# A list schedule that also holds the first stage, counts transfers by bytes and by how many are under way, and uses durations from a trace

## The chip, the cores and the metric

The kernel runs on one core of a Trainium2 chip. The metric is the device time of one execution in microseconds (us); lower is better. Engines: PE is TensorE, DVE VectorE, ACT ScalarE, POOL GpSimd, SP the engine that here only issues DMAs.

## The reference

One transformer layer of width 1024 on 1024 rows, batch 1, all in float32:

```python
u = rms_norm(h, g_norm_mix)
proj = einsum('btd,de->bte', u, w_in) + b_in
mq, mk, mv, mo, mi, mf, nq, nkv, ngate, merge = split_columns(proj, IN_SIZES)
y_m = mlstm_mixer(mq, mk, mv, mo, mi, mf, ...)      # 4 heads of 128, chunks of 128 rows
y_n = nsa_mixer(nq, nkv, ngate, pe_cmp, w_cmp1, w_cmp2, rel_bias)   # 8 heads of 64
branch = einsum('btnw,nwd->btnd', stack([y_m, y_n]), w_branch)
h = h + sum(sigmoid(merge) * branch) @ w_out
f = rms_norm(h, g_norm_ffn)
h = h + (silu(f @ w_gate) * (f @ w_up)) @ w_down
return rms_norm(h, g_final)
```

The mLSTM mixer puts a causal convolution of width 4 and a silu on q and k, works in 8 chunks per head with a running state, and multiplies each score by a decay that depends on the row, the column and the gates. The second mixer has compressed keys and values (blocks of 32 rows, stride 16, through a small two-layer network), selected blocks and a window, with a bias by distance.

## The kernel before, in words

**Products.** A float32 product is made from two halves: each operand is split into a high part (rounded) and the rest, and three matmuls (high·high, low·high, high·low; L343, L344, L345) are summed in PSUM. ACT writes the high part, DVE the low one.

**First stage (L413 to L577), written out by hand.** x comes in 8 tiles of 128 rows. norm(i) squares a tile and sums it on ACT (L458), works out the row's scale in a few one-column instructions (L353 to L360) and scales the tile on DVE (L462; in two halves for tiles 0 and 1). trans(i) transposes it in 8 matmuls of 128x128 (L467) into one PSUM tile and splits that into UTH and UTL (L340 is the low half): u, transposed, is what all later products read. p0(i) multiplies the tile by 288 columns of w_in in 24 matmuls. Those columns are 256 of V, 24 and 8 gate columns (MI); their weights come in 9 loads of SP, three for each group of rows (the tiles named raw), and are split in L325. p0_out adds the bias. The code of the loop at L546 fixes the order on every engine: trans(i+1), p0_out(i-1), norm(i+3), p0(i).

**The plan (class at L60, used from L583).** From there on nothing is in hand order. Code describes steps: on which engine, at which cost in ns, what buffers it reads and writes. Plan.run then picks, again and again, the step that can start first among the first few of each engine's list (the older one at a tie), by its own clocks, and issues it. The engines keep that order: each executes its own row of instructions, and waits in it. A step that depends on another engine's can start 190 ns (HOP) after its end, on PE another 500 ns (slack) later. A DMA costs SP 60 ns and lands a fixed 2,600 ns later (others 2,200 to 9,000), however large it is and however many are under way.

**What the plan holds.** The rest of the first stage (p0 of tile 7, and mv: the tile by 512 columns); twelve pairs of 128-column projections (PAIRS), each as seven products of 12 matmuls (Strassen's scheme, L343 to L345 with output bk), whose operands are formed in L703 and split in L594 and whose results are added up in L758 and L761; after each "qk" pair one mLSTM head; the gates; rel_rows (eight copies of a bias row to 128 partitions, d_rep, 960 KB each); compress.

**A head (L1030).** masks(cp) for each of four pairs of chunks loads two rows by row index, copied to 128 partitions: M from d_M and S from d_S (L1050, 128 KB each). L1052 makes the causal mask of M, L1054 copies the pair's decay out of S, another instruction scales q by S. st_a(c) is the score product (L1062) with an Exp on ACT and the product of both on DVE (L1072); st_b(c) holds the state's product (L1081) and the two of the output, pn (L1091, L1093). The pairs share two buffers: the load of pair 2 waits for the last reader of pair 0. When all chunks are done, norm_1 and norm_3 (L1116 to L1134, 11 small instructions), a scaling of the whole head (L594, RND) and 8 transposes on PE (L1144) follow. Mask rows, norm rows and the operands of later products stand in one row on DVE.

**Compress.** Two halves j. KX holds one half's keys in two shifted copies, loaded from d_kc by four DMAs (L1179, L1180); DVE and ACT copy strided columns of it out (L1196), which L1202 multiplies. The second half's load waits until the first half's copies have read KX, the first one's until the masks' buffers are free.

**After the plan** (PE from about 412 us on) come the attention, the merge and the FFN.

Of the kernel before, what the change touches and what calls it, by code (L numbers as in the profile page):

```python
# [65 lines left out]
class Plan:  # L66
# [4 lines left out]
    def __init__(self, banks, look=None, slack=0.0, **clock):  # L71
        self.LOOK, self.slack = look or self.LOOK, slack
        self.clock = dict({"PE": 0.0, "ACT": 0.0, "DVE": 0.0, "Pool": 0.0, "SP": 0.0}, **clock)
        self.todo = {e: [] for e in self.clock}
        self.at, self.n, self.boost = {}, 0, 0
        self.banks = [[ap, None] for ap in banks]
# [10 lines left out]
    def step(self, alts, fn, reads=(), writes=(), lat=0.0, after=0.0):  # L87
        deps = {d for b in reads for d in b.w} | {d for b in writes for d in b.w + b.r}
        for b in writes:
            if not b.w:  # L90
                for p in b.prior:
                    p.over = True
                    deps |= set(p.w + p.r)
        if any(b.over for b in (*reads, *writes)):
            raise RuntimeError("a region is used after it was given away")
        st = Step(alts, fn, deps, writes, lat, self.n - self.boost, after)
        self.n += 1
# [20 lines left out]
    def ready(self, st, eng, free, first):  # L118
        t = st.after
# [43 lines left out]
def body(ctx, tc, a, out):  # L163
# [16 lines left out]
    nc.scalar.activation(warm, eps, AF.Sqrt)  # L180
# [87 lines left out]
    d_M = tc.dram_tile([32, P], F32, name="d_M")  # L268
    d_S = tc.dram_tile([32, P], F32, name="d_S")
# [159 lines left out]
    BV = RMV()[:, 0:512]  # L429

    def load_x(i):
        nc.sync.dma_start(XS[i % 4], a["x"][P * i:P * i + P, :])

    load_x(0)
    load_x(1)
    nc.scalar.dma_start(gB, a["g_norm_mix"].partition_broadcast(P))
    nc.scalar.dma_start(cst, a["cst"].rearrange("p (n c) -> p n c", n=2))
    bin_ = a["b_in"]
    ws.dma(j_p0[-1])
    load_x(2)  # L440
    load_x(3)
    nc.gpsimd.dma_start(BB[:, 0:128], bin_[C_VS:C_VS + P].partition_broadcast(P))
    nc.gpsimd.dma_start(BB[:, 128:280], bin_[C_VW:C_VW + 152].partition_broadcast(P))
    nc.gpsimd.dma_start(BB[:, 280:288], bin_[C_MI:C_MI + 8].partition_broadcast(P))
    nc.gpsimd.dma_start(BV, bin_[C_MV:C_MV + 512].partition_broadcast(P))
    rv = lambda v, n: v.rearrange("(n c) -> n c", c=P)
    nc.gpsimd.dma_start(rows[0:16, :], rv(bin_[0:2048], 16))
    nc.gpsimd.dma_start(rows[16:20, :], rv(bin_[C_NQ:C_NQ + 512], 4))
    nc.gpsimd.dma_start(rows[20:26, :], rv(bin_[C_KV:C_KV + 768], 6))
    nc.gpsimd.dma_start(rows[26:42, :], rv(bin_[C_MG:C_MG + 2048], 16))  # L450
    nc.gpsimd.dma_start(rows[R_CV:R_CV + 32, :], a["conv_qk"].rearrange("j (n c) -> (j n) c", c=P))
    nc.gpsimd.dma_start(rows[R_GH:R_GH + 4, :], rv(a["g_mlstm_head"], 4))
    nc.gpsimd.dma_start(rows[R_PE:R_PE + 32, :], a["pe_cmp"].rearrange("j (o w) d -> (j o) (w d)", w=2))
    nc.gpsimd.dma_start(BF, a["b_fgate"].partition_broadcast(P))

    def norm(i):
        st, x_ = STA[i % 3], XS[i % 4]
        nc.scalar.activation(SQ, x_, AF.Square, accum_out=st[:, 0:1])  # L458
        rstd(st, D)
        for hf in range(2 if i < 2 else 1):  # L460
            ds_ = slice(512 * hf, 512 * hf + 512) if i < 2 else slice(0, D)
            nc.vector.scalar_tensor_tensor(x_[:, ds_], x_[:, ds_], st[:, 2:3], gB[:, ds_], ALU.mult, ALU.mult)  # L462

    def trans(i):
        pt = psT.tile([P, KT, P], F32, name=f"pt{i}", tag="pt", bufs=2)
        for k in range(KT):
            nc.tensor.transpose(pt[:, k, :], XS[i % 4][:, P * k:P * k + P], ident)  # L467
        if i + 4 < NT:
            load_x(i + 4)
        cs = slice(P * i, P * i + P)  # L470
        split_evict(UTH[:, :, cs], UTL[:, :, cs], pt)

    p0s = {}

    def p0_mm(i, ps):
        cs = slice(P * i, P * i + P)
        for k in range(KT):
            mm3(ps[:, 0:288], UTH[:, k, cs], UTL[:, k, cs], P0H[:, k, :], P0L[:, k, :], k == 0, k == KT - 1)

    def p0(i):  # L480
        p0s[i] = psT.tile([P, 512], F32, name=f"p0_{i}", tag="D", bufs=3)
        p0_mm(i, p0s[i])

    def p0_out(i, ps):
        vt, vs = VT[i % 2], VS[i % 2]
        nc.vector.tensor_tensor(vt, ps[:, 0:256], BB[:, 0:256], ALU.add)
        nc.vector.tensor_tensor(GT[:, i, :], ps[:, 256:288], BB[:, 256:288], ALU.add)
        v4 = vt.rearrange("p (n d) -> p n d", n=4)
        split_evict(vs[:, :, 0:64], vs[:, :, 64:128], v4)

    def mv_mm(i, ps):
        cs = slice(P * i, P * i + P)
        for k in range(KT):
            mm3(ps, UTH[:, k, cs], UTL[:, k, cs], MVW[0][k // 2][:, k % 2, :], MVW[1][k // 2][:, k % 2, :], k == 0, k == KT - 1)

    def mv_out(i, ps):
        nc.vector.tensor_tensor(MVS[i % 2], ps, BV, ALU.add)

    def v_store(i):
        nc.sync.dma_start(d_vhl[:, i], cast32(VS[i % 2]))  # L500

    def mv_store(i):
        nc.sync.dma_start(d_mv[:, :, i], MVS[i % 2].rearrange("p (h d) -> p h d", h=MH))


    RAWP = []
# [1855 lines left out]
```

## Time and profile before

| what | us |
|---|---|
| median of 3 runs | 1604.07 (1602.08 to 1604.45) |
| the profiled execution | 1605.79 |
| its span (first to last instruction) | 1603.9 |
| PE busy in it | 1536.7 |
| DVE, ACT, POOL busy | 1183.8, 785.5, 123.7 |
| first stage, by hand | about 0 to 58 |
| planned part | about 58 to 412 |

The busy time of an engine is the time in which at least one of its instructions ran; PE's instructions overlap, so a product's duration (0.39 us) is longer than its share of PE's time. "Idle before" in a row is the time for which the engine had nothing running, with what ended it: `<-DMA R<-d_M` is a load from d_M into the buffer R.

### The profile page before, as it was taken

Reading aid. Unit: us, or ns where it says so; the run is one execution under the profiler, and the core shown is the slowest. Engines: PE = TensorE matmul, PEld = TensorE weight load, DVE = VectorE, ACT = ScalarE, POOL = GpSimd, SP = SyncE. Lnnn points to the kernel's source line nnn. Section 1 sums busy time; section 2 is a strip of 40 time slices with the busy share of each in tenths; the row PEclk is TensorE's granted clock in tenths of the full one; section 3 lists DMA queues with packets and bytes.
Section 4 is the critical chain, followed back from the end, with each engine's and each line's share of the span. In section 5 each row is a group of like instructions: output and inputs, shape, how many; then the busy total and the mean of one; then the engine's idle time right before and its main releaser. Section 6 shows DMA issues by size and latency. Waiting matters only on the chain.

```text
span 1603.9 us, 22044 instructions
## 1 busy us (share of the span) xinstructions
PE 1536.7 (96%) x7714; PEld 1294.9 (81%) x7714; DVE 1183.8 (74%) x2448; ACT 785.5 (49%) x1664; POOL 123.7 (8%) x181
## 2 busy tenths in 40 slices
PE   6899989898999999998999989999999999999997
PEld 6778767787898988887787878888888888888876
DVE  6878787865798878785554488676576666978996
ACT  5336365553588868885444234333333333454433
POOL 1000000002110301001000022000000000000030
PEclk9999999999999999999999999999999999999999
DMA  6523556479623733217548212222332223741202
GB/s 209 171 75 94 172 173 199 127 193 233 152 58 95 124 85 101 67 33 273 157 138 269 73 66 88 84 80 92 119 92 79 79 79 116 278 162 49 95 11 105
DMA packets 168439, 198.22 MB, mean 124 GB/s; under 512 B 11432, under 2 KB 127590, under 8 KB 168328
## 3 DMA queue, kind: packets, MB, share of 16 engines
q1 hardware_dynamic: 156456, 183.10, 36.4%
q0 software_dynamic: 11536, 13.05, 5.1%
q8 instruction: 61, 1.00, 0.3%
q10 hardware_dynamic: 336, 0.66, 0.1%
q14 instruction: 50, 0.41, 0.1%
HBM read 146.34 MB, written 58.29 MB: 128 GB/s over the span
## 4 chain that ended last, share of the span: by engine, by line
PE 78%; DVE 10%; DMA 6%; ACT 3%; issue 2%; SPq 1%; POOL 0%; DVEq 0%; ACTq 0%
PE PS L344 15%; PE PS L345 15%; PE PS L343 15%; PE T L1498 4%; PE bk L343 3%; PE bk L345 3%; PE bk L344 3%; PE d L343 2%; PE obank L1520 2%; PE obank L1518 2%; PE d L345 2%; PE d L344 2%; PE br L345 2%; PE br L344 1%; PE br L343 1%
## 5 line engine op out<-in xcount | busy, mean ns | idle before, releaser
L1863 DVE TENSOR_TENSOR sl<-PS,sl 128x512 f32<-128x512 f32 x182 | 123.8, 687 | 98.0 <-PE PS L345 96.0
L1507 DVE TENSOR_TENSOR TL<-T,TH 128x512 fp32r<-128x512 f32 (+1 forms) x184 | 103.3, 581 | 28.7 <-ACT TH L1503 27.9
L1503 ACT ACTIVATE TH<-T 128x512 fp32r<-128x512 f32 (+1 forms) x184 | 90.3, 510 | 26.4 <-PE T L1498 23.4
L1863 DVE TENSOR_TENSOR sl<-sl,sl 128x512 f32<-128x512 f32 (+1 forms) x113 | 77.3, 690 | 17.1 <-ACT sl L1866 11.7
L1866 ACT ACTIVATE sl<-sl 128x512 f32<-128x512 f32 (+1 forms) x85 | 53.5, 631 | 70.9 <-PE PS L344 47.8
L343 PE MATMUL bk<-UTH,op 128*128 128x512 f32 x192 | 77.6, 404 | 1.7 <-ACT R L761 1.3
L1866 ACT ACTIVATE wh<-sl 128x512 fp32r<-128x512 f32 x61 | 38.4, 630 | 81.9 <-PE PS L344 71.6
L345 PE MATMUL bk<-UTH,op 128*128 128x512 f32 x192 | 75.1, 391 | 0.4 <-DVE op L594 0.4
L344 PE MATMUL bk<-UTL,op 128*128 128x512 f32 x192 | 75.0, 391 | 0.0
L343 PE MATMUL d<-UTH,whi 128*128 128x512 f32 x176 | 71.9, 408 | 1.3 <-ACT mg L1373 0.7
L345 PE MATMUL d<-UTH,wlo 128*128 128x512 f32 x176 | 69.2, 393 | 1.4 <-POOL wlo L325 1.4
L344 PE MATMUL d<-UTL,whi 128*128 128x512 f32 x176 | 69.0, 392 | 0.0
L343 PE MATMUL PS<-q 128*128 128x512 f32 x172 | 66.9, 389 | 0.0
L344 PE MATMUL PS<-q 128*128 128x512 f32 x172 | 66.9, 389 | 0.0
L345 PE MATMUL PS<-q 128*128 128x512 f32 x172 | 66.9, 389 | 0.0
L1866 ACT ACTIVATE q<-sl 128x512 fp32r<-128x512 f32 x74 | 43.4, 624 | 46.6 <-PE PS L344 29.1
L343 PE MATMUL bk<-T,op 128*128 128x512 f32 x144 | 59.3, 412 | 1.7 <-DVE S L758 1.7
L345 PE MATMUL bk<-T,op 128*128 128x512 f32 x144 | 56.9, 395 | 0.3 <-DVE op L594 0.3
L344 PE MATMUL bk<-T,op 128*128 128x512 f32 x144 | 56.7, 394 | 0.0
L345 PE MATMUL br<-YH,wlo 128*128 128x512 f32 x128 | 50.7, 396 | 2.5 <-POOL wlo L325 2.5
L343 PE MATMUL br<-YH,whi 128*128 128x512 f32 x128 | 50.4, 394 | 2.0 <-ACT whi L323 2.0
L1863 DVE TENSOR_TENSOR q<-sl,q 128x512 fp32r<-128x512 f32 x72 | 50.3, 735 | 2.7 <-ACT q L1866 2.6
(1381 smaller groups left out, 4845.9 us busy)
## 6 DMA issues: line engine op xcount, KB each, us to landing
ra<-in_w_gate SPq DMA_DIRECT2D x22, 512.0 KB, 3.8
d_gu<-sl SPq DMA_DIRECT2D x44, 256.0 KB, 2.1
rp<-in_w_in SPq DMA_DIRECT2D x17, 512.0 KB, 4.7
q<-d_mg SPq DMA_DIRECT2D x32, 256.0 KB, 3.5
d_rep<-d_row SPq DMA_DIRECT2D x8, 960.0 KB, 6.7
sl<-d_gu SPq DMA_DIRECT2D x15, 512.0 KB, 4.1
sl<-in_w_down SPq DMA_DIRECT2D x15, 512.0 KB, 4.3
raw<-in_w_in SPq DMA_DIRECT2D x13, 512.0 KB, 6.6
```

The source lines that it names most:

```text
L343: nc.tensor.matmul(ps, ah, bh, start=first, stop=False)
L344: nc.tensor.matmul(ps, ah, bl, start=False, stop=False)
L345: nc.tensor.matmul(ps, al, bh, start=False, stop=last)
L1498: nc.tensor.transpose(pt[:, z, P * r:P * r + P], e, ident)
L1503: nc.scalar.activation(hl[0][:, 0:m], pt[:, 0:m], AF.Copy)
L1507: nc.vector.tensor_tensor(hl[1][:, 0:m], pt[:, 0:m], cast32(hl[0])[:, 0:m], ALU.subtract)
L1518: nc.tensor.matmul(po, vv, th[:, z, :], start=(st[1] == 0), stop=False)
L1520: nc.tensor.matmul(po, vv, tl[:, z, :], start=False, stop=(st[1] == st[2]))
L1863: return pl.step(alts, lambda e: ENG[e].tensor_tensor(out_(), x(), y(), alu), reads, writes, **kw)
L1866: return pl.step((("ACT", cost),), lambda e: nc.scalar.activation(out_(), x(), fn), reads, writes, **kw)
```

## The change

All names are as before; lines moved down by some 10 to 20. The order of the work after the plan is the same on PE.

**The planner.** A DMA step now has a size (kb) and a number of DMAs (nd). It costs SP 400 ns each. Its landing is reckoned as the later of its issue + 1,500 ns and the landing before it, plus 4.1 ns per KB; and it may start only when the eighth one before it has landed. A step that follows another on its own engine (not PE) waits 105 ns instead of 60, PE's slack is 1,000 ns instead of 500, the lists are looked at further down, and the costs of most steps are replaced (norm_1 600 to 1,180, norm_3 420 to 1,020, the convolution 1,400 to 1,200).

```diff
     def ready(self, st, eng, free, first):
-        t = st.after
+        t = max(st.after, self.landed[st.nd - 9]) if st.nd else st.after
...
-            t = max(t, d.end + d.lat + (60.0 if d.eng == eng else self.HOP + self.slack * (eng == "PE")))
+            t = max(t, d.end + d.lat + ((60.0 if eng == "PE" else 105.0) if d.eng == eng else self.HOP + self.slack * (eng == "PE")))
...
             self.clock[e] = st.end
+            for k in range(st.nd):
+                t += st.alts[e] / st.nd
+                self.landed.append(max(t + 1500.0, self.landed[-1]) + st.kb / st.nd * 4.1)
+            if st.nd:
+                st.lat = self.landed[-1] - st.end
...
-    def dma(fn, reads=(), writes=(), lat=2600.0, **kw):
-        return pl.step((("SP", 60.0),), lambda e: fn(), reads, writes, lat=lat, **kw)
+    def dma(fn, reads=(), writes=(), kb=512.0, nd=1, **kw):
+        return pl.step((("SP", 400.0 * nd),), lambda e: fn(), reads, writes, kb=kb, nd=nd, **kw)
```

**The first stage as steps.** The plan is now made before it. A tile is transposed in two halves of four matmuls (L586), scaled in two halves (L572) and p0 and mv are in two halves of 12 matmuls. The weights of p0 come in three loads by SP (512, 456 and 152 KB) and, for the 8 MI columns, as one load that is Pool's first, 128x8x8 in 1,024 pieces of 32 bytes. cst (the identity) is loaded ahead of gB on ACT's queue; the ACT table load, formerly first, stands behind both.

```diff
-    nc.scalar.activation(warm, eps, AF.Sqrt)
...
+    nc.scalar.dma_start(cst, a["cst"].rearrange("p (n c) -> p n c", n=2))
     nc.scalar.dma_start(gB, a["g_norm_mix"].partition_broadcast(P))
-    nc.scalar.dma_start(cst, a["cst"].rearrange("p (n c) -> p n c", n=2))
+    nc.scalar.activation(warm, eps, AF.Sqrt)
...
+    gq.dma_start(MIR, wink[:, :, C_MI:C_MI + 8])
...
+    def w_mi():
+        hi, lo = P0H[:, :, 280:288], P0L[:, :, 280:288]
+        step1("ACT", 200.0, lambda: nc.scalar.activation(hi, MIR, AF.Copy), (), p0hb[3:], after=7000.0)
+        step1("DVE", 180.0, lambda: nc.vector.tensor_tensor(lo, MIR, cast32(hi), ALU.subtract), p0hb[3:], p0lb[3:])
...
+    for i in range(NT):
+        norm(i)
+        trans(i)
+        if i + 4 < NT:
+            xb(i + 4)
+        p0(i)
+        if i < 4:
+            w_mv(i)
+    cols()
+    for i in range(NT):
+        tail_mv(i)
```

PE's first rows, before (pt is the transposes' PSUM tile, p p0's output, T_0_109 and T_0_108 the split weights):

```order
1 L467 MATMUL pt_254<-cst,R_0_103 128x128 x8
2 L467 MATMUL pt_288<-cst,R_0_103 128x128 x8
3 L343 MATMUL p_0_308<-T_0_109,UTH 128x288
4 L344 MATMUL p_0_308<-T_0_108,UTH 128x288
5 L345 MATMUL p_0_308<-T_0_109,UTL 128x288
```

and now (bk are the plan's PSUM banks; L351 to L353 are the three matmuls):

```order
1 L586 MATMUL bk_228<-cst,R_0_102 128x128 x4
2 L586 MATMUL bk_229<-cst,R_0_102 128x128 x4
3 L351 MATMUL bk_230<-T_0_108,UTH 128x288
4 L352 MATMUL bk_230<-T_0_107,UTH 128x288
5 L353 MATMUL bk_230<-T_0_108,UTL 128x288
```

p0 of tile 0 now stands ahead of the transposes of tile 1, which come behind its 24 matmuls. On DVE, before, from the end of tile 0's statistics (R_0_103 holds x, RSM the row statistics; L462 scales, L340 makes the low half of u, L325 that of the weights from raw):

```order
6 L360 TENSOR_TENSOR RSM_106<-RSM_106 128x1
7 L462 SCALAR_TENSOR_TENSOR R_0_103<-R_0_103,RSM_106,T_0_107 128x512 x2
8 L353 TENSOR_SCALAR RSM_106<-RSM_106 128x1
9 L357 RECIPROCAL RSM_106<-RSM_106 128x1
10 L358 SCALAR_TENSOR_TENSOR RSM_106<-RSM_106 128x1
11 L359 TENSOR_SCALAR RSM_106<-RSM_106 128x1
12 L360 TENSOR_TENSOR RSM_106<-RSM_106 128x1
13 L462 SCALAR_TENSOR_TENSOR R_0_103<-R_0_103,RSM_106,T_0_107 128x512 x2
14 L340 TENSOR_TENSOR UTL<-pt_254,UTH 128x8x128
15 L325 TENSOR_TENSOR T_0_108<-raw_210,T_0_109 128x864
16 L325 TENSOR_TENSOR T_0_108<-raw_214,T_0_109 128x864
17 L325 TENSOR_TENSOR T_0_108<-raw_218,T_0_109 128x576
```

and now (L572 scales, L591 makes the low half of u, L547 that of the weights from rp, and L552 that of the MI columns, which lie in RSM):

```order
6 L368 TENSOR_TENSOR RSM_105<-RSM_105 128x1
7 L552 TENSOR_TENSOR T_0_107<-RSM_105,T_0_108 128x8x8
8 L572 SCALAR_TENSOR_TENSOR R_0_102<-R_0_102,RSM_105,T_0_106 128x512 x2
9 L567 TENSOR_SCALAR RSM_105<-RSM_105 128x1
10 L591 TENSOR_TENSOR UTL<-bk_228,UTH 128x4x128
11 L591 TENSOR_TENSOR UTL<-bk_229,UTH 128x4x128
12 L547 TENSOR_TENSOR T_0_107<-rp_201,T_0_108 128x8x128
13 L365 RECIPROCAL RSM_105<-RSM_105 128x1
14 L366 SCALAR_TENSOR_TENSOR RSM_105<-RSM_105 128x1
```

The scaling of tile 1 moved behind tile 0's splits and the weights, and L552, which waits for Pool's load of the MI columns, stands ahead of the first scaling.

**Masks.** d_M and d_S are one DRAM tensor, d_MS, and one load per pair of chunks (L1065, 256 KB) takes the place of two (L1050): it writes both halves of the buffer, and so starts when M's reader and S's readers are both done.

```diff
-            for d_, ap, b in ((d_M, MB, mbb[cp]), (d_S, SB, sbb[cp])):
-                r0 = d_[h + 8 * cp:h + 8 * cp + 1, :]
-                dma(lambda r0=r0, ap=ap: nc.sync.dma_start(ap(cp), bass.AP(tensor=r0.tensor, offset=r0.offset, ap=[[0, P], [4 * P, 2], [1, P]])),
-                    [dms], [b], lat=2600.0)
...
+            r0 = d_MS[h + 8 * cp:h + 8 * cp + 1, :]
+            dma(lambda: nc.sync.dma_start(by(half(10, cp % 2), 2), bass.AP(tensor=r0.tensor, offset=r0.offset, ap=[[0, P], [8 * P, 2], [1, 2 * P]])),
+                [dms], [mbb[cp], sbb[cp]], kb=512.0)
```

SP's row where head 0's first masks are loaded, before (L503 stores mv, R_0_103 is the masks' buffer):

```order
37 L503 DMA d_mv<-RND_104 512x1x128 x5
38 L886 DMA d_M<-S_0_100 32x128
39 L887 DMA d_S<-S_0_100 32x128
40 L1050 DMA R_0_103<-d_M 128x2x128
41 L1050 DMA R_0_103<-d_S 128x2x128
42 L1050 DMA R_0_103<-d_M 128x2x128
43 L1050 DMA R_0_103<-d_S 128x2x128
44 L503 DMA d_mv<-RND_104 512x1x128
```

and now (L642 stores mv, L477 loads weights of a pair):

```order
33 L642 DMA d_mv<-RND_103 512x1x128 x4
34 L904 DMA d_MS<-S_0_99 32x256
35 L642 DMA d_mv<-RND_103 512x1x128
36 L1065 DMA R_0_102<-d_MS 128x2x256 x2
37 L477 DMA rp_202<-in_w_in 128x4x128 x2
38 L477 DMA rp_203<-in_w_in 128x4x128 x2
39 L642 DMA d_mv<-RND_103 512x1x128
```

Four loads became two, one behind the other. In PE's row, the number of 128x512 product matmuls between the pn product that frees a pair's buffer and the state's product (L1081, now L1096) that needs the next content of it was 18 in heads 0 to 2; now it is 54, 42, 30 and 30 in heads 0 to 3. Between the last pn of a head and the head's transposes (L1144, now L1159) there were 30 in each head; now there are 36. Between the first and the second half of compress there are 24 in both.

DVE's row at the norm of head 2, before (L758 adds up a product, L703 forms an operand, L1054 and L1052 belong to the next head's masks):

```order
431 L703 SCALAR_TENSOR_TENSOR op_662<-S_0_102,op_662 128x512
432 L1054 COPY RSM_106<-R_0_103 128x2
433 L1052 TENSOR_TENSOR R_0_103<-cst,R_0_103 128x256
434 L1116 SCALAR_TENSOR_TENSOR RSM_106<-RND_104 128x8
435 L1117 TENSOR_TENSOR RSM_106<-RSM_106,ECOL 128x8
436 L1118 RECIPROCAL RSM_106<-RSM_106 128x8
```

and now (L721 forms an operand, L494 and L1009 are an operand's sum and the convolution, L1067 and L1069 belong to the next masks):

```order
445 L1067 TENSOR_TENSOR R_0_102<-cst,R_0_102 128x2x128
446 L1069 COPY RSM_105<-R_0_102 128x2
447 L494 TENSOR_TENSOR S_0_101<-rp_202,S_0_101 128x512
448 L1009 SCALAR_TENSOR_TENSOR S_1_1165<-R_0_102,COLS,S_1_1165 128x1023
449 L721 SCALAR_TENSOR_TENSOR op_236<-S_0_99,op_236 128x512
450 L1131 SCALAR_TENSOR_TENSOR RSM_105<-RND_103 128x8
451 L1132 TENSOR_TENSOR RSM_105<-RSM_105,ECOL 128x8
```

The rows of the next masks moved from directly ahead of the norm to three rows further up, with longer work between.

**Other transfers.** compress loads KX by two DMAs instead of four for each half, and the second-layer weights by two instead of four. rel_bias is loaded by Pool instead of ACT. The stores of d_b12 are separate steps. rel_rows is described ahead of finish(0), so ahead of head 0, instead of behind it, and its rows have four buffers instead of two.

```diff
+                if n == 0:
+                    rel_rows()
                 finish(x[0])
                 nm, j = PAIRS[x[0]]
                 if nm == "qk":
                     head(j)
-        if n == 0:
-            rel_rows()
...
-                for g in range(2):
-                    src = d_kc[j][64 * g:64 * g + 64, :]
-                    nc.sync.dma_start(KX()[0:64, g, :], src)
-                    nc.sync.dma_start(KX()[64:128, g, 0:T - 1], src[:, 1:T])
-            dma(go, [dkc], [kxb[j]], lat=5000.0)
+                src = d_kc[j].rearrange("(g p) t -> p g t", g=2)
+                nc.sync.dma_start(KX()[0:64, :, :], src)
+                nc.sync.dma_start(KX()[64:128, :, 0:T - 1], src[:, :, 1:T])
+            dma(go, [dkc], [kxb[j]], kb=1024.0, nd=2)
```

In all, SP has 29 DMA issues fewer of 556.

More of the change, by code (lines that the diff above doesn't have):

```diff
@@ L85, in buf, with trail, step @@
         return b
-    def step(self, alts, fn, reads=(), writes=(), lat=0.0, after=0.0):
+    def trail(self, b):
+        return set(b.w + b.r) if b.w else set(b.r).union(*(self.trail(p) for p in b.prior))
+    def step(self, alts, fn, reads=(), writes=(), lat=0.0, after=0.0, kb=0.0, nd=0):
         deps = {d for b in reads for d in b.w} | {d for b in writes for d in b.w + b.r}
@@ L267, in body @@
     d_rep = [tc.dram_tile([P, RW], F32, name=f"d_rep{h}") for h in range(NH)]
-    d_M = tc.dram_tile([32, P], F32, name="d_M")
-    d_S = tc.dram_tile([32, P], F32, name="d_S")
+    d_MS = tc.dram_tile([32, 2 * P], F32, name="d_MS")
     d_mv = tc.dram_tile([P, MH, NT, MD], F32, name="d_mv")
@@ L456, in norm @@
[L456 to L506, printed above, removed]
+    gq = nc.gpsimd
@@ new lines, in norm @@
+    def norm(i):
+        st, x_ = STA[i % 3], XS[i % 4]
+        sb = stb[i] = pl.buf([("st", i % 3)], True)
+        v = nc.vector
+        step1("ACT", 1150.0, lambda: nc.scalar.activation(SQ, x_, AF.Square, accum_out=st[:, 0:1]), bx[i], [sb, sqb])
+        step1("DVE", 100.0, lambda: v.tensor_scalar(st[:, 0:1], st[:, 0:1], 1.0 / D, EPS, ALU.mult, ALU.add), (), [sb])
+        step1("ACT", 130.0, lambda: nc.scalar.activation(st[:, 1:2], st[:, 0:1], AF.Sqrt), (), [sb])
+        step1("DVE", 730.0, lambda: rstd_b(st), (), [sb])
+        for z in range(2):
+            ds_ = slice(512 * z, 512 * z + 512)
+            step1("DVE", 605.0, lambda ds_=ds_: v.scalar_tensor_tensor(x_[:, ds_], x_[:, ds_], st[:, 2:3], gB[:, ds_], ALU.mult, ALU.mult),
+                  [sb, gbb], [bx[i][z]], after=7500.0)
@@ new lines, in utile, with trans, go @@
+    def utile(i, z=None):
+        j, r = divmod(i, 2)
+        return [ub[q, j] for q in ((1, 2), (4, 3))[r]][slice(None) if z is None else slice(z, z + 1)]
+    def trans(i):
+        cs = slice(P * i, P * i + P)
+        for z in range(2):
+            pt = pl.buf()
+            def go(z=z, pt=pt):
+                for k in range(4):
+                    nc.tensor.transpose(pt.ap[:, P * k:P * k + P], XS[i % 4][:, 512 * z + P * k:512 * z + P * k + P], ident)
+            step1("PE", 650.0, go, [bx[i][z]], [pt], after=8000.0)
+            hi, lo = UTH[:, 4 * z:4 * z + 4, cs], UTL[:, 4 * z:4 * z + 4, cs]
+            v = lambda pt=pt: by(pt.ap, 4)
+            step1("ACT", 587.0, lambda hi=hi, v=v: nc.scalar.activation(hi, v(), AF.Copy), [pt], utile(i, z))
+            step1("DVE", 605.0, lambda hi=hi, lo=lo, v=v: nc.vector.tensor_tensor(lo, v(), cast32(hi), ALU.subtract), [pt], utile(i, z))
@@ L629, in tail_mv @@
+    mvsb = [pl.buf((), True) for z in range(2)]
     def tail_mv(i):
```

322 lines of the change are left out of this document (164 added, 158 removed).

## The prediction, made before the result was known

> **What bounds the kernel now.** I read the page's chain of waits first, then busy time by stage, then what TensorE (PE) waits for in the stages that the change touches, and last the rows at the longest waits. The chain that ended last, by engine, from the page:
>
> ```profile
> PE 78%; DVE 10%; DMA 6%; ACT 3%; issue 2%; SPq 1%; POOL 0%; DVEq 0%; ACTq 0%
> ```
>
> TensorE bounds it, and the change removes no product, so its busy time stays. Only its idle time can go, and the 22% of the chain on other engines are mostly that idle time. Where does it lie? The windows, first column the stretch in us, second its length, then busy time by engine, PE's granted clock, DMA share and GB/s:
>
> ```profile
> 0.00:60.00 60.00, 41.59 (x261) 39.15 (x262) 42.29 (x98) 29.54 (x50) 7.37 (x20) 0.97 0.63 191
> 60.00:200.00 140.00, 138.45 (x637) 110.83 (x636) 115.02 (x218) 58.10 (x115) 0.66 (x2) 1.00 0.42 123
> 200.00:300.00 100.00, 85.11 (x433) 70.14 (x432) 78.19 (x159) 55.31 (x130) 0.00 (x0) 0.98 0.56 175
> 300.00:412.00 112.00, 106.11 (x520) 88.96 (x519) 70.84 (x135) 54.53 (x109) 16.48 (x28) 0.97 0.90 205
> 412.00:1604.00 1192.00, 1165.44 (x5871) 985.87 (x5869) 877.45 (x1840) 588.07 (x1261) 99.22 (x131) 0.99 0.35 108
> ```
>
> PE idles 18.4 us in the first 60 (the first stage), 1.6 from there to 200, 14.9 in 200 to 300 (heads 1 and 2), 5.9 in 300 to 412 (head 3, compress), and 26.6 after 412, where the order of work is the same in both kernels. So 41 us can be argued about, and the change reorders the work of all 41. What PE waits for, first in the front, then in the planned part (us, times, longest):
>
> ```profile
> PE pt L467 <- DMA cst<-in_cst: 9.2, 1, 9.2
> PE pt L467 <- DVE R L462: 4.0, 4, 1.3
> PE p L345 <- DVE UTL L340: 3.4, 3, 1.7
> PE pt L467 <- DVE S L462: 1.3, 1, 1.3
> ```
>
> ```profile
> PE bk L1081 <- DVE S L1072: 5.9, 3, 3.1
> PE bk L1144 <- DVE RND L594: 4.6, 2, 3.9
> PE bk L1202 <- DVE S L1196: 4.4, 1, 4.4
> PE bk L343 <- DVE S L758: 1.7, 1, 1.7
> PE bk L343 <- ACT R L761: 1.3, 1, 1.3
> ```
>
> All but two name VectorE (DVE). But DVE is 78% busy in 200 to 300: it waits itself, in its own order. What for, in 200 to 330, and how long the mask loads (L1050) take:
>
> ```profile
> DVE RSM L1054 <- DMA R<-d_S: 13.0, 6, 4.5
> DVE R L1052 <- DMA R<-d_M: 6.4, 4, 4.0
> ```
>
> ```profile
> DMA to landing us min/median/max: 3.0/4.6/7.4
> ```
>
> So behind ten stops of PE's helper stands one kind of transfer. DVE's rows before the longest wait of L1144 show the chain: a mask that isn't needed yet holds up a head's norm behind it.
>
> ```profile
> 284.60 0.42 DVE L1052 TENSOR_TENSOR R<-cst,R 128x256 f32<-128x256 f32 x1 [3.97 <-DMA R<-d_M]
> 284.94 0.16 DVE L1116 SCALAR_TENSOR_TENSOR RSM<-RND 128x8 f32<-128x8 f32 x1
> ```
>
> **The change, part by part.** The working is made against the profiled execution, 1605.8 us (span 1603.9); the median shown, 1604.1, is 1.7 lower, which I take off at the end.
>
> *Masks (L1081).* A chunk pair's buffer is free when its last pn product has read it; then SP issues the load, it lands, DVE and ACT work on it, and L1081 of the pair after next may run. That needs about 0.4 (an issue of SP, like the 0.45 further down) + 4.6 to 7.4 (landing, the row above) + some 1.4, an estimate (L1052's 0.42 in the last rows, the Exp and the product, costed at 0.29 and 0.21 in the diff, and as much for the hops between them). I take 5.7 for the landing, between median and maximum because 256 KB now come where 128 did: 7.5 us. The cover is the products between. One costs 0.23 (start to start in the two rows in the middle here; the outer ones serve below):
>
> ```profile
> 366.38 5.49 PE L1202 MATMUL bk<-S,S 128*128 128x126 f32 x24 [4.44 <-DVE S L1196]
> ...
> 372.92 0.40 PE L344 MATMUL bk<-UTL,op 128*128 128x512 f32 x1
> 373.15 0.39 PE L345 MATMUL bk<-UTH,op 128*128 128x512 f32 x1
> 373.38 1.05 PE L1202 MATMUL bk<-S,S 128*128 128x126 f32 x8
> ```
>
> Before, 18 products stood there, 4.1 us. Now 54, 42, 30 and 30 stand in heads 0 to 3: 12.2, 9.5, 6.8, 6.8. Heads 0 and 1 are covered, heads 2 and 3 miss 0.7 each. Of 5.9 go **4.5**. The halves must now both be free before one load may start, the Exp's on ACT and pn's on PE; the later one decides in both.
>
> *A head's norm (L1144).* The next head's mask no longer stands directly ahead of the norm, so the stop of 3.97 isn't passed on; 36 products instead of 30 stand between the last pn and the transposes. I keep the shorter wait, 4.6 - 3.9 = 0.7, and 0.3 for DVE's other work: **3.6** go.
>
> *Product waits (L343).* Its 1.7 + 1.3 are late evictions. True durations in the planner (norm 1,180 and 1,020 ns instead of 600 and 420) and a slack of 1,000 ns for PE should remove some. Bounds 0 and 3.0; I take half, **1.5**.
>
> *Compress (L1202).* The second half's load waits for the first half's reads, in both kernels with 24 products (5.5 us) of cover. SP issues four loads one after the other, of which this is the first; two instead save about 2 x 0.45 = 0.9:
>
> ```profile
> 354.24 0.45 SPq L1179 DMA_DIRECT2D R<-d_kc  x1
> ```
>
> Bounds 0 and 4.4: I take the middle, **2.2**.
>
> *Slow clock after idling.* After the longest stops PE is slow for a while:
>
> ```profile
> 289.71 1.25 PE L1144 MATMUL bk<-cst,RND 128*128 128x128 f32 x8 [3.88 <-DVE RND L594]
> 290.61 0.78 PE L343 MATMUL bk<-T,op 128*128 128x512 f32 x1
> ...
> 294.05 0.40 PE L345 MATMUL bk<-T,op 128*128 128x512 f32 x1
> ```
>
> ```profile
> 271.46 0.49 PE L1081 MATMUL bk<-RMV,S 128*128 128x129 f32 x2 [3.09 <-DVE S L1072]
> ```
>
> From 290.61 to 294.05 eight products take 3.44 instead of 8 x 0.23 = 1.82: 1.6 lost, 0.2 more in L1144 itself. L1202 took 5.49 for 24 against 3 x 1.05: 2.3, and 0.5 in the products behind. After 3.09 idle nothing was lost. So **1.8** come back with L1144's wait, and of compress's 2.8 half, **1.4**.
>
> The Trainium skill (TensorE: Matmul & The Clock Gate, Part 1, the HAM clock gate) says that the clock halves after an idle window of about 3.4 us. The trace agrees: 3.88 and 4.44 were followed by slow rows, 3.09 wasn't. By that rule a compress wait of 2.2 loses nothing, so all 2.8 would come back, and the forecast would be 1.4 lower.
>
> *The front.* No product goes. The front's three later rows of waits, 8.7 us, are a ceiling. DVE sets the pace; first its waits for the square of a tile on ACT, then rows of its time:
>
> ```profile
> DVE RSM L353 <- ACT T L458: 10.1, 7, 5.2
> ```
>
> ```profile
> 7.36 1.41 DVE L462 SCALAR_TENSOR_TENSOR R<-R,RSM,T 128x512 f32<-128x512 f32 x2
> 9.98 0.15 DVE L353 TENSOR_SCALAR RSM<-RSM 128x1 f32<-128x1 f32 x1 [1.22 <-ACT T L458]
> ...
> 19.04 1.28 DVE L462 SCALAR_TENSOR_TENSOR R<-R,RSM,T 128x1024 f32<-128x1024 f32 x1
> ```
>
> Of the 10.1 the first, 5.2, is the start itself. Of the 4.9 behind it the first 1.2 stays (DVE's second tile still comes right behind its first); the other 3.7 can be filled with splits of other tiles. Against that, six more tiles are scaled in halves (1.41 - 1.28 = 0.13 each, 0.8), and a DVE row that waits for the MI columns now stands ahead of the first scaling. Those columns come in 1,024 pieces as Pool's first transfer; the nearest rows are the old loads that held the MI columns, 12 KB each, 8.9 us to landing behind other loads, and a load of Pool's at the start, 6.8:
>
> ```profile
> T<-in_b_in POOLq DMA_DIRECT2D x1, 76.0 KB, 6.8
> ...
> raw<-in_w_in SPq DMA_DIRECT2D x2, 12.0 KB, 8.9
> ```
>
> ```profile
> 1.26 0.74 POOL L442 DMA_DIRECT2D T<-in_b_in  x1 [0.81 <-POOLq L2350]
> ```
>
> Issued at about 1.3, when Pool's first load was, it lands between 8.1 and 10.2, where scaling began at 7.36: 0.7 to 2.8 late, of which the first wait for cst, 9.2, covers some. I take **2.0** for the front (3.7 - 0.8 - 0.9), between -1 and 8.7.
>
> The Trainium skill (DMA: Bandwidth & Descriptors, Specifications) wants pieces of at least 512 B for full rate; these have 32. That speaks against this part; taken with the 8.9 row as the price, the front would gain 0.9 instead of 2.0. Nothing here shows such a transfer alone.
>
> *At nothing:* fewer issues on SP (29 rows fewer), w2's two loads instead of four, the table load behind ACT's DMAs, rel_rows before finish(0): SP and ACT aren't PE's releaser there, and the eight copies of 960 KB (d_rep) now lie between the masks of heads 0 and 1 instead of 1 and 2, where the DMA share is 0.42 and 0.56. If that cover is gone, they delay masks, which is the second and third case below.
>
> *Sum:* 4.5 + 3.6 + 1.5 + 2.2 + 1.8 + 1.4 + 2.0 = 17.0 us. But thousands of rows change places, and new waits will appear that no row shows. The five rows of the old order's planned part hold 17.9 us; with costs nearer to the traced ones I allow a third, 6.0. Net 11.0: 1605.8 - 11.0 = 1594.8, and 1.7 less for the median: **1593**.
>
> **Rivals.** *No new waits:* the allowance of 6.0 isn't used: 1587; with the front's whole 8.7, 1580. For it speaks the longer cover at every mask, against it that DVE's rows are no fewer, 78% busy where the waits lie.
>
> *The waits only move:* the same bytes pass the same queue, so whichever load is planned earlier pushes another one back, and DVE stops as long in total. Only the front's 2.0 stay: 1602, no change by this kernel's measure (3.2 us, 0.2%, is about what can be told). The mask loads' spread of 3.0 to 7.4 speaks for it.
>
> *Slower:* the merged mask load lands late in DVE's row. With the longest landing, 7.4, and 0.4 of issue and 1.4 behind it, the need is 9.2 against 6.8 of cover in heads 2 and 3: 2.4 for each of their four later loads, 9.6. As DVE stops in order, the terms that hang on it (masks, norm, evictions, compress) aren't gained either: 1605.8 + 9.6 - 2.0 - 1.7 = 1612. It decides if the load takes over about 6.5 us as a rule; that old loads had a median of 4.6 speaks against it.
>
> **How the numbers follow.** The forecast 0.60, no new waits 0.15, moved waits 0.13, slower 0.12. The low end, 1580, takes in the second case with most of the front's ceiling; the high end, 1606, takes in the third case even if the front loses 1 instead of gaining 2, 1605. Faster by over 0.2% is the first two cases, 0.75.
>
> **What would show it.** PE idle in 200 to 300 falls from 14.9 to under 8; no L1159 (the old L1144) wait above 1; DVE's waits for the mask loads in 200 to 330 fall from 19.4 to under 8; PE's clock there 1.00; the front's last p0 ends 1 to 4 us earlier. It is wrong if the mask loads land after 6.5, if DVE's waits for DMA are as long as before, or if stage C, the same in order, is what moved.

## The result and the profile after

The changed kernel takes 1573.62 us (median of 4 runs, 1572.64 to 1576.46) against 1603.07 of before: ratio 0.9821, 95% interval 0.9802 to 0.9839. Forecast were 1593 and a range from 1580 to 1606; the direction was right, the size was 11 us forecast and 29 measured. The profiled execution took 1576.46 us, with a span of 1574.7 against 1603.9.

The chain that ended last, by engine, on the page of after:

```profile
PE 85%; DVE 7%; DMA 5%; ACT 2%; issue 1%; SPq 0%; POOL 0%; DVEq 0%; ACTq 0%; POOLq 0%
```

PE's part rose from 78% to 85%. The windows of after, cut where its stages end (attention starts some 30 us earlier, so 382 stands for 412):

```profile
0.00:60.00 60.00, 44.94 (x288) 41.33 (x289) 47.77 (x123) 30.09 (x60) 8.74 (x22) 1.00 0.74 232
60.00:200.00 140.00, 139.24 (x648) 112.01 (x647) 119.82 (x231) 66.87 (x130) 0.67 (x2) 1.00 0.43 134
200.00:300.00 100.00, 100.00 (x531) 85.60 (x530) 86.39 (x178) 62.52 (x150) 0.00 (x0) 1.00 0.55 172
300.00:382.00 82.00, 79.30 (x401) 66.11 (x400) 49.55 (x103) 34.22 (x68) 19.36 (x33) 1.00 1.08 236
382.00:1575.00 1193.00, 1166.13 (x5854) 986.19 (x5853) 871.62 (x1838) 588.33 (x1261) 97.97 (x127) 0.99 0.35 108
```

PE's idle time fell from 18.4 to 15.1 in the first 60 us, from 14.9 to nothing in 200 to 300, and from 5.9 to 2.7 behind that. Its waits in after, the four longest of the first 60 us, and then all from 60 to 390:

```profile
PE bk L586 <- DVE R L572: 9.8, 1, 9.8
PE bk L351 <- ACT T L546: 3.0, 1, 3.0
PE bk L352 <- DVE T L547: 1.1, 1, 1.1
PE bk L586 <- DVE S L572: 0.9, 1, 0.9
```

```profile
PE bk L351 <- ACT S L779: 1.6, 1, 1.6
PE bk L879 <- DVE RSM L874: 0.8, 1, 0.8
PE d L351 <- ACT op L1349: 0.5, 1, 0.5
PE d L353 <- DVE op L494: 0.5, 1, 0.5
```

No row is left of L1096 (once L1081), L1159 (L1144) or L1216 (L1202): the waits of the masks, the norm and compress are gone whole, not in part. Behind that, DVE's stops for masks fell from 15.8 + 8.7 to 1.5 us, though a load lands no earlier (median 4.7 instead of 4.6). Who waited for the loads of L1050, before:

```profile
  DVE RSM L1054: 15.8, 8
  DVE R L1052: 8.7, 6
```

and for those of L1065, after:

```profile
  DVE R L1067: 1.5, 2
...
DMA to landing us min/median/max: 4.4/4.7/7.2
```

DVE's time at the norm of head 2 answers to the rows where it stood 3.97 us. The mask is subtracted without a wait, and the norm comes behind other work:

```profile
265.81 0.42 DVE L1067 TENSOR_TENSOR R<-cst,R 128x256 f32<-128x256 f32 x1
266.14 0.16 DVE L1069 COPY RSM<-R 128x2 f32<-128x2 f32 x1
...
268.61 0.17 DVE L1131 SCALAR_TENSOR_TENSOR RSM<-RND 128x8 f32<-128x8 f32 x1
```

**Where the 29.2 us of the span come from.** The first matmul of the attention (S1w) starts at 383.9 instead of 417.3, 33.4 earlier; 1,872 matmuls stand before it in both. PE idled 18.5 us up to there instead of 40.7, so 22.2 of it are waits. The other 11.2 are PE's busy time: 365.3 for the same matmuls instead of 376.5. The granted clock, here its mean over 20 us, shows most of that. Before:

```profile
40.00:60.00 20.00, 15.02 (x97) 13.99 (x96) 16.64 (x38) 9.13 (x15) 0.00 (x0) 0.91 0.57 158
280.00:300.00 20.00, 16.12 (x69) 13.05 (x68) 14.61 (x30) 7.39 (x12) 0.00 (x0) 0.91 0.48 130
360.00:380.00 20.00, 15.56 (x75) 13.36 (x74) 10.22 (x21) 10.06 (x17) 2.64 (x5) 0.83 0.78 190
```

It was 0.91, 0.91 and 0.83 in these stretches and is 1.00 in every 20 us of after up to 380: (0.09 + 0.09 + 0.17) x 20 = 7.0 us. Cut closer, it is about half there: 0.51 in 51.5 to 55.0, 0.52 in 290.6 to 294.0 and 0.50 in 365.6 to 372.4. (The 1.00 of the first 20 us is no proof of full speed: in both kernels the p0 matmuls start 0.24 us apart up to about 20.5 us and 0.13 apart from 22 us on.) Also each stop costs about 0.16, an estimate, in which a last matmul runs out (0.39 against 0.23 in the stream), and stops over 0.3 us fell from 23 to 7: 2.6. The remaining 1.6 isn't accounted for.

Then 4.2 us are given back: the attention takes 1190.8 us instead of 1186.7, since its first selected scores (S1s) wait for DVE and DVE for a bias load (d_rep). That load went out 1.0 us ahead of S1w (382.8), behind two stores in SP's row, and landed 6.1 us later; before, it went out 2.9 ahead (414.3), and DVE didn't wait. Behind the stop the clock is slow again, and the matmuls start 0.43 us apart instead of 0.23:

```profile
390.22 0.76 PE L1430 MATMUL S1s<-S,S 128*128 128x512 f32 x1 [2.94 <-DVE nx L1457]
390.78 0.63 PE L1431 MATMUL S1s<-S,S 128*128 128x512 f32 x1
391.21 0.63 PE L1430 MATMUL S1s<-S,S 128*128 128x512 f32 x1
```

```profile
380.00:400.00 20.00, 17.03 (x80) 13.95 (x79) 13.15 (x53) 10.10 (x34) 1.84 (x7) 0.83 0.31 106
```

```profile
389.06 0.82 DVE L1457 CUSTOM_DVE_ANT_0 E1w<-S1w,FW 128x640 f32<-128x640 f32 x1 [2.98 <-DMA FW<-d_rep]
```

So half of the 7.0 us of clock comes back here: 0.17 x 20 = 3.4. Stop and slow clock together cost 5.3: from the first S1w on, the same matmuls take 12.0 us instead of 6.7.

### The profile page after: what moved, and what is told of

Its sections match the earlier page's. It is cut to its first block, busy times and chain, and to the rows that moved or that the text cites. A ratio compares the mean times of both kernels' runs of the same rounds, so it can differ in the third digit from the quotient of the medians.

```text
span 1574.7 us, 22067 instructions
## 1 busy us (share of the span) xinstructions
PE 1529.6 (97%) x7714; PEld 1291.2 (82%) x7714; DVE 1175.1 (75%) x2467; ACT 782.0 (50%) x1668; POOL 126.7 (8%) x184
## 4 chain that ended last, share of the span: by engine, by line
PE 85%; DVE 7%; DMA 5%; ACT 2%; issue 1%; SPq 0%; POOL 0%; DVEq 0%; ACTq 0%; POOLq 0%
PE PS L352 15%; PE PS L353 15%; PE PS L351 15%; PE bk L351 4%; PE bk L352 4%; PE bk L353 4%; PE T L1512 4%; PE obank L1534 2%; PE d L351 2%; PE obank L1532 2%; PE d L353 2%; PE d L352 2%; PE br L353 2%; PE br L351 2%; PE br L352 2%; DMA d_ql<-S 1%
## 5 line engine op out<-in xcount | busy, mean ns | idle before, releaser
L351 PE MATMUL bk<-UTH,op 128*128 128x512 f32 x192 | 77.5, 403 | 1.6 <-ACT S L779 1.6
L353 PE MATMUL bk<-UTH,op 128*128 128x512 f32 x192 | 75.1, 391 | 0.0
L351 PE MATMUL d<-UTH,whi 128*128 128x512 f32 x176 | 71.9, 409 | 1.4 <-ACT mg L1387 0.7
L353 PE MATMUL d<-UTH,wlo 128*128 128x512 f32 x176 | 69.3, 394 | 1.4 <-POOL wlo L333 1.4
L351 PE MATMUL PS<-q 128*128 128x512 f32 x172 | 67.0, 390 | 0.0
L353 PE MATMUL PS<-q 128*128 128x512 f32 x172 | 67.0, 390 | 0.0
L351 PE MATMUL bk<-T,op 128*128 128x512 f32 x144 | 58.3, 405 | 0.0
L353 PE MATMUL bk<-T,op 128*128 128x512 f32 x144 | 56.4, 391 | 0.0
L351 PE MATMUL br<-YH,whi 128*128 128x512 f32 x128 | 50.8, 397 | 2.2 <-ACT whi L331 2.2
L353 PE MATMUL br<-YH,wlo 128*128 128x512 f32 x128 | 50.8, 397 | 2.2 <-POOL wlo L333 2.2
L1877 DVE TENSOR_TENSOR wh<-sl,wh 128x512 fp32r<-128x512 f32 x58 | 39.7, 685 | 15.3 <-ACT wh L1880 15.3
```

What stands on the lines that cost most here:

```text
L351: nc.tensor.matmul(ps, ah, bh, start=first, stop=False)
L353: nc.tensor.matmul(ps, al, bh, start=False, stop=last)
L1877: return pl.step(alts, lambda e: ENG[e].tensor_tensor(out_(), x(), y(), alu), reads, writes, **kw)
```

## The experiments

**How they are read.** Each ratio is to runs of the kernel before on the same chip in the same job. "Lead" is how much more matmul work PE has done than in the kernel before at the same moment of the profiled runs: each matmul that has started counts its columns at the full-speed 512 per 0.2267 us (the spacing of 0.23 above). The last column is by how much the attention starts earlier than before's 417.3.

| run | us | ratio | lead at 60 | 150 | 200 | 300 | attention earlier |
|---|---|---|---|---|---|---|---|
| changed kernel | 1573.6 | 0.9821 | 6.1 | 5.4 | 6.6 | 24.0 | 33.4 |
| b_model | 1580.3 | 0.9860 | 0.5 | 0.2 | -0.5 | 16.5 | 23.5 |
| b_lat2 | 1582.6 | 0.9872 | 0.5 | 0.0 | -0.2 | 13.0 | 21.6 |
| b_plan | 1588.2 | 0.9889 | 0.5 | 0.6 | -1.8 | 10.3 | 18.0 |
| front_only | 1602.4 | 0.9990 | 5.0 | 5.8 | 0.9 | 2.0 | -0.1 |
| front_slack | 1587.4 | 0.9899 | 5.8 | 7.0 | -1.8 | 3.4 | 12.0 |
| fixed_landing | 1576.9 | 0.9825 | 6.2 | 4.6 | -1.0 | 16.5 | 25.3 |
| fixed_rel_late | 1580.4 | 0.9872 | 6.7 | 6.0 | 6.1 | 16.3 | 23.1 |
| rel_late | 1587.7 | 0.9905 | 6.3 | 6.9 | -1.4 | 16.0 | 19.8 |
| old_costs | 1565.4 | 0.9760 | 6.3 | 6.5 | 6.1 | 23.4 | 36.7 |

The theories: A, the planner now knows when transfers land; B, there are fewer and larger transfers; C and F, the first stage is in the plan; D, the place of rel_rows.

**Fewer, larger transfers.** b_masks is the kernel before with the merged mask load; two_masks the changed kernel with two loads again:

```diff
-            dma(lambda: nc.sync.dma_start(by(half(10, cp % 2), 2), ...), [dms], [mbb[cp], sbb[cp]], kb=512.0)
+            for s, ap, b in ((0, MB, mbb[cp]), (1, SB, sbb[cp])):
+                dma(lambda s=s, ap=ap: nc.sync.dma_start(ap(cp), ...), [dms], [b], kb=256.0)
```

> The kernel before with one mask load per pair instead of two and nothing else. Theory A: no gain, 1599 to 1607, DVE's stops for masks stay above 12 us. Theory B: 1580 to 1592, and the stops fall under 8 us.

> The changed kernel with two mask loads of 128 KB per pair again, everything else as changed. Theory A: the order already allows for their landing, 1572 to 1578. Theory B: 1585 to 1600, with mask stops of DVE back above 10 us.

Measured 1603.4 (0.9997, 0.9985 to 1.0008) and 1574.5 (0.9819, 0.9792 to 0.9846). DVE's stops, of b_masks and of two_masks (the lines of the masks' subtraction):

```profile
  DMA R<-d_MS: 21.1, 10
```

```profile
  DMA R<-d_MS: 1.2, 2
```

Half as many loads without the new order stop DVE as long; as many loads as before in the new order don't stop it. Theory B falls for the masks. The merged KX loads were not tried by themselves; the runs below that keep four of them (b_model, b_lat2) gain without the merging.

**The planner's rules on the old kernel.** b_plan has all of them, as the change's diff shows them, b_model the lines on landed, kb and nd and the longer look-ahead, b_costs the durations and the slack alone, b_lat2 only this:

```diff
-        return pl.step((("SP", 60.0),), lambda e: fn(), reads, writes, lat=lat, **kw)
+        return pl.step((("SP", 60.0),), lambda e: fn(), reads, writes, lat=2.0 * lat, **kw)
```

> The kernel before with the new planner rules alone (transfers by bytes and eight under way, traced durations, slack 1,000); first stage by hand, two mask loads per pair and four KX loads as before. Theory A, the order made from true landings and durations took the waits away: PE's waits from 200 to 412 fall from 20 us to under 6, time 1578 to 1584 (the front's share of some 5 us is missing). Theory B, fewer and larger transfers did it: 1598 to 1604, DVE still stops some 15 us for mask loads. Theory C, the first stage in the plan did it: 1595 to 1603.

> The kernel before with the landing model alone (bytes, eight under way, 400 ns of SP per DMA); old durations, slack 500, first stage by hand, rel_rows late. Theory A: as the run with all planner rules, 1584 to 1592, DVE's stops for masks from 24 us down to some 5. If model and durations are needed together: 1597 to 1605.

> The kernel before with the new durations and the slack of 1,000 alone; fixed landings, first stage by hand, two mask loads. If durations and slack carry what the rules alone gained (1588 with landing model and durations together): 1585 to 1592. If the landing model carries it: 1598 to 1606.

> The kernel before with all fixed landing times of DMAs doubled (masks 5,200 instead of 2,600 ns) and nothing else. If it is enough that the planner takes landings to be late (measured 4.6 us for the masks), whatever their size: 1578 to 1592, DVE's mask stops under 8 us. If the sizes and the queue behind each other are what matters: 1596 to 1606.

Measured: b_plan 1588.2 (0.9861 to 0.9917), b_model 1580.3 (0.9845 to 0.9874), b_costs 1605.3 (0.9996 to 1.0020), b_lat2 1582.6 (0.9855 to 0.9888). b_plan fell between what theories A and C expected, and b_model gained more than its expectation. The landing model alone gains 22 us on the old kernel, and old times taken twice gain 20; their intervals overlap. So neither the bytes nor the queue are needed for it: it is enough that all of SP's DMAs are taken to land later, a mask after 5.2 us, when it lands after some 4.6, instead of after 2.6. The limit of eight under way does nothing at all: without it, not one instruction stands elsewhere in the order, in b_model or in the changed kernel, and the longer look-ahead moves none on the kernel before either. The stops of DVE for masks in b_model and b_lat2:

```profile
  DMA R<-d_M: 2.2, 2
```

```profile
  DMA R<-d_S: 7.4, 3
```

Durations and slack alone gain nothing. Added to the model (b_plan) they took 8 us off its gain by the medians, but the intervals of the two ratios overlap.

**Parts undone in the changed kernel.** fixed_landing puts the old 60 ns and fixed times back behind the first stage; old_costs the old durations there; slack500 and slack900 change one number.

```diff
+        if fixed:
+            return pl.step((("SP", 60.0),), lambda e: fn(), reads, writes, lat=lat, **kw)
         return pl.step((("SP", 400.0 * nd),), lambda e: fn(), reads, writes, kb=kb, nd=nd, **kw)
```

```diff
-        step1("DVE", 1180.0, norm_1, [nd, colg], [ssb])
+        step1("DVE", 600.0, norm_1, [nd, colg], [ssb])
...
-        step1("DVE", 1020.0, norm_3, (), [ssb])
+        step1("DVE", 420.0, norm_3, (), [ssb])
```

```diff
-              {"PE": 160, "SP": 120, "ACT": 260, "DVE": 400, "Pool": 200}, 1000.0, ACT=2300.0, DVE=1000.0, SP=750.0, Pool=14000.0)
+              {"PE": 160, "SP": 120, "ACT": 260, "DVE": 400, "Pool": 200}, 900.0, ACT=2300.0, DVE=1000.0, SP=750.0, Pool=14000.0)
```

> The changed kernel, but in the planned part behind the first stage a DMA costs SP 60 ns and lands after the old fixed times. Theory A with the landing model as its main part: PE's waits in the planned part come back to 12 us or more, 1588 to 1600. Theory A with the durations as its main part, or theories B and C: 1572 to 1580.

> The changed kernel with the old durations of compute steps in the planned part (norm_1 600, norm_3 420, convolution 1,400 and so on); landing model, slack and first stage as changed. If the durations are the main part of theory A: PE's waits from 60 to 412 above 10 us, 1584 to 1596. If landing and durations each suffice alone, or the slack does it: 1572 to 1579.

> The changed kernel with PE's slack at 500 ns instead of 1,000. If the slack carries the gain (steps on PE are put 1 us behind their inputs, so lateness of any kind is absorbed): 1582 to 1595. If not: 1572 to 1578.

> The changed kernel with a slack of 900 instead of 1,000, a change with no meaning of its own. If orders of this planner scatter by chance: more than 4 us off 1574, either way. If the rules determine the time: 1571 to 1577.

Measured: fixed_landing 1576.9 (0.9803 to 0.9847), old_costs 1565.4 (0.9734 to 0.9786), slack500 1569.4 (0.9759 to 0.9802), slack900 1568.3 (0.9750 to 0.9794). Two things follow. A slack of 900, which means nothing, moved the time by 5 us, more than "the rules determine the time" allowed: orders of this planner scatter, and the changed kernel is at the slow end of its neighbours. And old_costs is faster than the changed kernel, the intervals of their ratios lie apart: traced durations were no help to an order that already knew its landings. It beats both kernels. Most of this scatter can be read from the traces: it lies in one load. Up to the attention old_costs is 3.3 us ahead of the changed kernel and slack900 0.9; but their bias load goes out 2.9 and 2.8 us ahead of S1w instead of 1.0, and they have neither the stop of 2.94 nor the slow clock behind it, which cost 5.3. slack500, like old_costs faster than either case that was expected for it, has a stop of 2.3 there. That fixed_landing lost only 3 us spoke against theory A as the only cause, and led to the next runs.

**The place of rel_rows.** b_rel is the kernel before with rel_rows early; rel_late the changed kernel with it late; fixed_rel_late has fixed landings as well.

```diff
-                if n == 0:
-                    rel_rows()
                 finish(x[0])
...
+        if n == 0:
+            rel_rows()
         if n == 8:
             compress()
```

> The kernel before with rel_rows described ahead of head 0 and nothing else. Theory D, the eight 960 KB copies between the masks of heads 1 and 2 were what made those late: 1585 to 1595, PE's lead over before grows by some 8 us or more between 200 and 300. Theory A, the planner must know the landing: 1600 to 1608.

> The changed kernel with rel_rows behind head 0 again; landing model as changed. Theory A: the model puts the masks where they land in time wherever the copies are, 1566 to 1577. Theory D: 1582 to 1592.

> The changed kernel with both undone: fixed landings in the planned part, rel_rows behind head 0. If either of the two is enough alone (1577 with fixed landings and rel_rows early): the waits of heads 1 and 2 come back, 1588 to 1598. If neither matters much and the first stage in the plan carries the gain: 1574 to 1580.

Measured: b_rel 1604.1 (0.9994 to 1.0024), rel_late 1587.7 (0.9891 to 0.9920), fixed_rel_late 1580.4 (0.9844 to 0.9899). rel_late missed A's expectation: 14 us lost, a time that theory D expected. Nearly half is one stop, told by its rows on SP, ACT and PE:

```profile
178.77 10.73 SPq L985 DMA_DIRECT2D d_row<-S  x4
189.59 0.34 SPq L1040 DMA_DIRECT2D d_kh<-S  x1
190.82 0.57 SPq L987 DMA_DIRECT2D d_rep<-d_row  x1
191.48 0.55 SPq L1041 DMA_DIRECT2D d_kl<-S  x1
```

```profile
198.25 0.69 ACT L779 ACTIVATE S<-bk,COLS 128x512 f32<-128x512 f32 x1 [4.80 <-DMA d_kl<-S]
```

```profile
198.99 0.80 PE L351 MATMUL bk<-T,op 128*128 128x512 f32 x1 [6.63 <-ACT S L779]
```

rel_rows' four stores hold SP for 10.7 us, 9.4 of it waiting for DVE's copies of rows that PE makes; behind them in SP's row stand the stores that free the buffer which ACT writes next, and PE waits for ACT. Stops of 6.3 to 7.0 at the same place (about 200 us) are in b_plan, front_slack and fixed_old_costs, all with rel_rows late. Not every late order has it (b_model and fixed_rel_late don't), and no run with the early place does. The other half of the 14 us isn't traced. With fixed landings the late place costs no more than 4 us (fixed_rel_late against fixed_landing, overlapping intervals). That the stop isn't theory D's (copies delaying masks) shows in rel_late's mask stops: 1.7 us.

**The first stage.** These join edits shown above. front_only keeps it in the plan and undoes the rest behind it (fixed landings, old durations, slack 500, two mask loads, four KX loads, late rel_rows; the 105 ns, the look-ahead and Pool's costs stay new); front_slack has a slack of 1,000 on top. b_costs_masks has durations, slack and merged masks and the old first stage. fixed_slack500 and fixed_old_costs are fixed_rel_late with the old slack or the old durations.

> The changed kernel with everything undone behind the first stage: fixed landings, old durations, slack 500, two mask loads, four KX loads, rel_rows behind head 0. Left are the first stage in the plan and the small edits of transfers beside it. Theory F, one plan from the first instruction gives the planned part true clocks and thereby most of the gain even without the landing model: 1576 to 1585, PE's lead over before grows by some 10 us or more between 200 and 300. Theory G, the first stage is worth its own 6 us and the rest comes from the planner's rules: 1594 to 1601.

> The kernel before with new durations, slack 1,000 and one mask load per pair, fixed landings, first stage by hand. If durations and merged masks only work together (each alone gave nothing): 1580 to 1592. Theory F and the landing model as the only two causes: 1600 to 1607.

> The first stage in the plan with everything behind it undone (1602 so), but PE's slack at 1,000. If first stage and slack together are enough: 1577 to 1587. If durations or merged masks are needed as well: 1594 to 1605.

> The changed kernel with fixed landings, rel_rows late (1580 so) and PE's slack back at 500; durations, merged masks and KX loads as changed. If the slack is what covers late landings where the model is missing: 1592 to 1603. If not: 1576 to 1585.

> The changed kernel with fixed landings, rel_rows late (1580 so) and the old durations; slack 1,000, merged masks and KX loads as changed. If the traced durations are what helps where the model is missing: 1592 to 1603. If not: 1575 to 1585.

Measured: front_only 1602.4 (0.9979 to 1.0002), b_costs_masks 1600.9 (0.9976 to 1.0001), front_slack 1587.4 (0.9883 to 0.9916), fixed_slack500 1596.9 (0.9937 to 0.9967), fixed_old_costs 1586.3 (0.9873 to 0.9911). front_only fits neither theory: it has its lead of 5 to 6 us up to 150 and only 1 to 2 at 200 and 300. It meets the old waits, at other places and as long:

```profile
PE bk L1166 <- DVE RND L494: 10.1, 2, 5.3
PE bk L351 <- ACT R L785: 4.4, 1, 4.4
```

Where the planner takes landings to be early, it is the slack that helps: 15 us between front_only and front_slack, 13 (by the ratios) to 16 between fixed_slack500 and fixed_rel_late, each more than the scatter; the durations' 3 to 6 (fixed_old_costs against fixed_rel_late) are within it, the intervals overlap, and its time lies between its two cases. Where it knows the landings, the slack gives nothing (slack500). Why the same slack gives nothing with the hand-written first stage (b_costs, b_costs_masks) stays open. So late landings in the planner are enough on the kernel before, but in the changed kernel no one of the landing model, the durations, the slack and the merged masks is needed: without it the time is 1565 to 1577. Only the place of rel_rows cost more when undone (1588).

## Why the prediction was wrong, point by point

**The sum.** The span fell by 29.2: 22.2 of waits and 11.2 of busy time, less the 4.2 given back. The forecast had 13.8 of waits and 3.2 of slow clock, less 6.0 for new waits: 11.0. So it missed 8.4 in the waits, 8.0 in the busy time and 1.8 in what is given back. The step that failed is the sizing of these terms, the slow clock's most of all, and of the waits the rests that were left standing; the mechanism stood.

**Masks, norm, compress.** The mechanism was right: loads that land later than planned stop DVE, and DVE's order passes it on. I had 4.5 of 5.9, 3.6 of 4.6 and 2.2 of 4.4; all of 5.9, 4.6 and 4.4 went. I left rests because I took 5.7 us for the landing, which made heads 2 and 3 short of cover, kept 1.0 of the norm's for DVE's other work, and took "the middle" for compress. The landing was 4.7. These rests make 4.6 of the 8.4; the small rows of waits behind the five that I listed, 4.4 before and 1.8 after, make 2.6, and the front 1.3.

**Product waits.** 1.5 forecast; of 3.0 a new one of 1.6 (L351 for ACT) stays: 1.4.

**Slow clock.** The most mis-sized term: 3.2 forecast, against 11.2 us less of busy time on the same matmuls, 7.0 of it granted clock. I had counted only the rows right behind two stops, and half of the second. The windows of before showed 0.91 in 40 to 60, 0.91 in 280 to 300 and 0.83 in 360 to 380; my working used only the long ones (0.97, 0.98, 0.97), where the same loss looks small. The rule drawn on, that a stop of 3.09 us costs nothing and one of 3.88 does, isn't borne out either: the slow stretch from 51.5 on began behind a stop of 1.65, the last of several, and in after a stop of 2.94 was followed by 6 us of slow matmuls.

**The front.** 2.0 forecast; PE idles 3.3 us less in the first 60, and with the faster clock of 40 to 60 it has a lead of 6.1 at 60 us. The MI columns did land late, 7.3 us after their issue at 1.3, and DVE's first scaling slid from 7.36 to 9.02 behind them, as worked out:

```profile
8.88 0.23 DVE L552 TENSOR_TENSOR T<-RSM,T 128x64 fp32r<-128x64 f32 x1 [1.47 <-ACT T L551]
9.02 1.41 DVE L572 SCALAR_TENSOR_TENSOR R<-R,RSM,T 128x512 f32<-128x512 f32 x2
```

The last p0 ends 0.7 us earlier (58.6 instead of 59.4), less than the 1 to 4 that I named as a sign. What I missed is that the plan puts mv between the p0, work that before began at 59.2 us; it is the row L351 (and two like it) of PE's groups in the first 60 us:

```profile
L351 PE MATMUL bk<-S,UTH 128*128 128x512 f32 x11 | 4.4, 400 | 0.0
L353 PE MATMUL bk<-S,UTL 128*128 128x512 f32 x10 | 3.9, 395 | 0.0
L352 PE MATMUL bk<-S,UTH 128*128 128x512 f32 x10 | 3.9, 393 | 0.0
```

31 x 0.227 = 7.0 us, where before had four of them up to 60: the 27 more are the lead of 6.1. A moved stage is to be costed by what may run beside it, not by its own end. Fewer issues, which I put at nothing, may have helped here too: SP took 10.4 us over nine weight loads and issued the third x tile at 12.1; three loads took 6.2, and it went out at 7.9. That was not tried by itself.

**The allowance for new waits** (-6.0) came out near its size by luck. It was meant for the planned part, since I took the new order to be as prone to waits as the old; there it has only the new 1.6 and two of 0.5. What was given back, 4.2, lies in the attention, which I had said would not move.

**rel_rows at nothing** was wrong: its place is worth 14 us in the changed kernel (rel_late), though nothing on the kernel before (b_rel). Nearly half of it is SP's order and not the copies; the rest isn't traced.

**The rivals.** "No new waits" was nearest (1587, with the front's ceiling 1580); what it lacks is the 8.4 of waits and the 8.0 of busy time, less the 4.2 given back. "The waits only move" is what front_only and b_masks did: 1602 and 1603. "Slower" asked for landings over 6.5; the median is 4.7.

## What to carry to other kernels

In a list schedule, an assumed landing that is too short puts a consumer where its engine stands still, and everything behind it in that engine's order waits with it: compare the assumed times with the page's issue-to-landing first, and err to the late side (doubling them gained 20 us here). Refinements beyond that (bytes instead of doubled times, traced durations) moved no more than the scatter of orders, some 5 to 8 us here, and the limit on transfers under way nothing, so try a few neighbours of a setting before one is credited, and read where they part: here it was mostly one load, that the stage behind the plan needs, issued 1.9 us later. Price a stop with the slow clock behind it, read in short windows, and look at what stands behind a waiting DMA issue in SP's row.

## What the runs showed of the hardware

A stop of PE cost more than its length: with 22.2 us of idle time went 11.2 us of busy time on the same 1,872 matmuls, 7.0 of them by granted clocks of 0.83 to 0.91 over 20 us. In windows of 3.4 to 6.9 us at these places the clock was 0.50 to 0.54, and the stop ahead of it was 1.65, 3.88, 4.44 and, in after, 2.94 us long, while one of 3.09 had none behind it: the length of the stop alone didn't tell. The merged mask load of 256 KB landed in the same median time (4.7 us) as the loads of 128 KB (4.6).
